# Adaptive max pool, 1-D: a fixed ring of 48 KB load slots and one extra load over 16 partitions, in place of slots that shrink from 64 KB to 48 KB

## The chip, the cores and the metric

One core of one Trainium2 chip. The metric is device microseconds of one execution. The kernel before was run three times: 335.7, 335.65 and 335.5 us, median 335.65 us. The profiled execution is one of its own kind: it took 335.7 us, of which 333.9 us are the span from its first instruction to its last.

## What is computed

`x` is 32 x 256 x 4096 float32 (134.2 MB), the output 32 x 256 x 256 float32 (8.4 MB). Each output is the maximum of 16 neighbouring inputs, since 4096 / 256 = 16:

```python
batch, channels, length = x.shape            # 32, 256, 4096
for i in range(output_size):                 # 256
    start = int(i * length / output_size)
    end = int((i + 1) * length / output_size)
    result[:, :, i] = np.max(x[:, :, start:end], axis=-1)
```

So `x` can be read as one long row of 2,097,152 windows of 16 floats (64 bytes), each of which gives one float (4 bytes).

## The kernel before

The long row of windows is cut into two groups, and each group into 128 equal pieces, one for each partition. A partition then owns 16,384 windows: 8,784 of the first group and 7,600 of the second. In what follows a "column" is one window on each of the 128 partitions: 64 bytes of each partition to load, 4 bytes to store.

A load (L74) brings some columns to one of three slots of the tile `area`; VectorE (DVE) reduces that slot with one `reduce_max` (L75) into the output part at the end of the same tile; the slot is then free for the third load after it. Memory of a partition is one area of 53,200 floats which slots and outputs share. The outputs grow downward from its end, and the slots get what is left, so they shrink: three loads each of 1,024, 980, 924, 868, 816 and 768 columns, and a last one of 244 (the loop at L43 to L50 works these sizes out). That is 19 loads. A load of 1,024 columns is 65,536 bytes to each partition, one of 768 columns is 49,152.

All DMAs are issued by SyncE (SP) in program order: 19 loads, then three stores (L91). The first store takes the whole first group (8,784 columns); the second takes the first six loads of the second group (5,052 columns), the third its last four loads (2,548 columns, L86 to L88). A load waits at SP until the reduce of the load three before it is done; the last store waits for the last reduce. VectorE does nothing but the 19 reduces, and the other engines compute nothing.

Of the kernel before, what the change touches and what calls it, by code (L numbers as in the profile page):

```python
# [1 line left out]

# [4 lines left out]


@with_exitstack
def kernel(  # L10
    ctx: ExitStack,
    tc: tile.TileContext,
    x: bass.AP,
    output_size: bass.AP,
    out: bass.AP,
):

    nc = tc.nc
    P = nc.NUM_PARTITIONS
    fp32 = mybir.dt.float32

    B, C, L = x.shape
    O = int(output_size)
    assert L % O == 0, (L, O)
    W = L // O
    total = B * C * O // P  # L30
    assert B * C * O % P == 0

    AREA = 53200
    SLOTS = 3
    MOST = 65536 // (4 * W)
    ALIGN = 4
    ROUNDS_A = 3
    LAST = 4


    sizes = []
    left = total
    while left:  # L43
        room = AREA - (total - left)
        n = min(room // (SLOTS * W + SLOTS) // ALIGN * ALIGN, MOST)
        for _ in range(SLOTS):
            n = min(n, left)
            if n:
                sizes.append(n)
                left -= n  # L50
    groups = [sizes[: ROUNDS_A * SLOTS], sizes[ROUNDS_A * SLOTS :]]

    pool = ctx.enter_context(tc.tile_pool(name="pool", bufs=1))
    area = pool.tile([P, AREA], fp32, tag="area", name="area")

    xw = x.flatten_outer_dims().rearrange("r (o w) -> (r o) w", w=W)
    ow = out.flatten_outer_dims().rearrange("r o -> (r o)")

    stores = []
    n_loads = 0  # L60
    first = 0
    low = AREA
    for g, loads in enumerate(groups):
        n = sum(loads)
        xg = xw[first : first + P * n].rearrange("(p n) w -> p (n w)", p=P)
        og = ow[first : first + P * n].rearrange("(p n) -> p n", p=P)
        first += P * n
        base = low - n
        b = n
        for i, size in enumerate(loads):  # L70
            a = b - size
            at = n_loads % SLOTS * sizes[n_loads // SLOTS * SLOTS] * W
            slot = area[:, at : at + size * W]
            nc.sync.dma_start(out=slot, in_=xg[:, a * W : b * W])  # L74
            nc.vector.reduce_max(  # L75
                out=area[:, base + a : base + b],
                in_=slot.rearrange("p (n w) -> p n w", w=W),
                axis=mybir.AxisListType.X,
            )
            n_loads += 1  # L80
            b = a
        low = base
        if g == 0:
            stores.append((og, area[:, base : base + n]))
        else:
            end = sum(loads[len(loads) - LAST :])  # L86
            for a, b in ((end, n), (0, end)):
                stores.append((og[:, a:b], area[:, base + a : base + b]))  # L88

    for dst, src in stores:  # L90
        nc.sync.dma_start(out=dst, in_=src)  # L91


# [1 line left out]
_INS = ['x', 'output_size']  # L95
_OUTS = [((32, 256, 256), 'float32')]

_NUMBERS = {'output_size': 256}


# [26 lines left out]
```

## Time and profile before

| what | value |
|---|---|
| median of three runs | 335.65 us |
| profiled execution, whole | 335.7 us |
| profiled execution, span of its instructions | 333.9 us |
| VectorE busy | 276.0 us (83% of the span), 19 reduces |
| VectorE idle before its reduces | 50.0 us, all of it waiting for a load |
| read from and written to device memory | 134.22 MB and 8.39 MB |
| mean rate over the span | 427 GB/s |

The DMA work of the core is done by 16 DMA engines. A DMA is cut into packets, which are spread over them; the profile counts packets, bytes and the share of the 16 engines' time that packets took. Each DMA tells its end with increments of a semaphore, one from each of the 16 engines, and the trace keeps the time of every one of them. A view by windows gives, for any stretch of time, what VectorE did and what the DMA engines moved; a packet is counted there whole in the window in which it starts.

### The profile page before, as it was taken

What the parts mean: (1) busy time and instruction counts of PE and PEld (TensorE: products, weight loads), DVE (VectorE), ACT (ScalarE), POOL (GpSimd) and SP (SyncE); (2) the same over time, 40 slices, a digit from 0 to 9 for tenths busy, and PEclk for the clock granted to TensorE, in tenths of its full rate; (3) what the DMA queues carried; (4) which work ended last, traced back from release to release, by engine and by line L of the source; (5) the groups of instructions that cost most, each with busy time, mean ns of one, the idle gap of its engine ahead of it and who ended that gap; (6) DMA issues with size and microseconds to landing.
All of it is one profiled execution on the core that took longest, in us unless ns stands there. A gap on an engine that the chain in (4) does not pass through costs nothing.

```text
span 333.9 us, 109 instructions
## 1 busy us (share of the span) xinstructions
DVE 276.0 (83%) x19; POOL 0.2 (0%) x4
## 2 busy tenths in 40 slices
DVE  0029899798979899897979897979989798988990
POOL 0000000000000000000000000000000000000000
DMA  9898989998999998999999999999999998998997
GB/s 377 377 502 377 495 385 471 392 473 376 473 443 398 474 439 383 425 453 453 446 426 433 426 426 426 426 425 469 407 419 475 395 465 389 465 436 383 448 420 311
DMA packets 3168, 142.61 MB, mean 427 GB/s; under 512 B 352, under 2 KB 352, under 8 KB 352
## 3 DMA queue, kind: packets, MB, share of 16 engines
q1 hardware_dynamic: 3168, 142.61, 99.1%
HBM read 134.22 MB, written 8.39 MB: 427 GB/s over the span
## 4 chain that ended last, share of the span: by engine, by line
DMA 63%; DVE 34%; another core or an unknown queue 1%; issue 0%; SPq 0%
DMA area<-in_x_dram 63%; DVE area L75 34%; SPq L74 0%
## 5 line engine op out<-in xcount | busy, mean ns | idle before, releaser
L75 DVE TENSOR_REDUCE area<-area 128x1024 f32<-128x16384 f32 (+6 forms) x19 | 276.0, 14525 | 50.0 <-DMA area<-in_x_dram 50.0
L108 POOL MEMSET const-bfloat16-1.0<- 128x1 bf16 x1 | 0.1, 102 | 0.0
L108 POOL MEMSET const-uint8-127<- 128x1 uint8 x1 | 0.1, 101 | 0.0
L108 POOL MEMSET const-float32-0.0<- 128x1 f32 x1 | 0.1, 100 | 0.2 <-issue 0.2
L108 POOL MEMSET const-float32-1.0<- 128x1 f32 x1 | 0.1, 99 | 0.0
## 6 DMA issues: line engine op xcount, KB each, us to landing
area<-in_x_dram SPq DMA_DIRECT2D x3, 7840.0 KB, 39.1
area<-in_x_dram SPq DMA_DIRECT2D x3, 7392.0 KB, 36.9
area<-in_x_dram SPq DMA_DIRECT2D x3, 6944.0 KB, 34.7
area<-in_x_dram SPq DMA_DIRECT2D x3, 6528.0 KB, 32.6
area<-in_x_dram SPq DMA_DIRECT2D x3, 6144.0 KB, 30.7
out_dram<-area SPq DMA_DIRECT2D x1, 4392.0 KB, 30.7
out_dram<-area SPq DMA_DIRECT2D x1, 2526.0 KB, 36.3
area<-in_x_dram SPq DMA_DIRECT2D x1, 1952.0 KB, 20.7
```

The lines of the kernel that those rows point to most:

```text
L75: nc.vector.reduce_max(out=area[:, base + a : base + b], in_=slot.rearrange("p (n w) -> p n w", w=W), axis=mybir.AxisListType.X,)
L108: nc = _bacc.Bacc("TRN2", target_bir_lowering=False, num_devices=1)
```

## The change

The shrinking slots are replaced by a ring of three slots of fixed size, 760 columns (48,640 bytes to each partition). Ahead of the two groups, 6,144 windows are taken off as a side piece: 16 partitions of 384 windows (24,576 bytes) each. The rest is 16,336 columns of 128 partitions, in groups of 7,600 and 8,736 columns: 10 loads of 760, then 11 of 760 and a last one of 376. The side load stands in the middle, as the twelfth of 23 (`SIDE_AT = 11` loads go before it). It is issued as two DMAs, one over 15 partitions and one over the sixteenth, and reduced by one instruction over 16 partitions. The columns are now walked from low to high. The stores are four: 7,600 columns, the side piece, 7,600 columns and 1,136 columns; the last one holds the last two loads. As built, SP has 24 load DMAs and 4 store DMAs where it had 19 and 3, and VectorE 23 reduces where it had 19. In the built program both sides of the sixteenth partition's DMA are one contiguous run of 6,144 floats: the `(k n)` view with `k=16` in the source does not survive the building.

```diff
-    AREA = 53200
     SLOTS = 3
-    MOST = 65536 // (4 * W)
-    ALIGN = 4
-    ROUNDS_A = 3
-    LAST = 4
...
-    while left:
-        room = AREA - (total - left)
-        n = min(room // (SLOTS * W + SLOTS) // ALIGN * ALIGN, MOST)
-        for _ in range(SLOTS):
-            n = min(n, left)
-            if n:
-                sizes.append(n)
-                left -= n
-    groups = [sizes[: ROUNDS_A * SLOTS], sizes[ROUNDS_A * SLOTS :]]
+    CHUNK = 760
+
+    SIDE_P, SIDE, SIDE_AT = 16, 384, 11
+    rest = (total - SIDE_P * SIDE) // P
+    GROUPS = [10 * CHUNK, rest - 10 * CHUNK]
+    CUT = 10 * CHUNK
...
-    area = pool.tile([P, AREA], fp32, tag="area", name="area")
+    ring = pool.tile([P, SLOTS, CHUNK * W], fp32, tag="ring", name="ring")
...
+    def next_slot(parts, n):
+        nonlocal n_loads
+        slot = ring[0:parts, n_loads % SLOTS, 0 : n * W]
+        n_loads += 1
+        return slot
+
+    def pooled(dst, src):
+        nc.vector.reduce_max(
+            out=dst,
+            in_=src.rearrange("p (n w) -> p n w", w=W),
+            axis=mybir.AxisListType.X,
+        )
+
+    def load(dst, src, a, b):
+        slot = next_slot(P, b - a)
+        nc.sync.dma_start(out=slot, in_=src[:, a * W : b * W])
+        pooled(dst[:, a:b], slot)
+
+    xs, os_ = group(SIDE_P, SIDE)
+    side_out = pool.tile([SIDE_P, SIDE], fp32, tag="side", name="side")
+
+    def load_side():
+        slot = next_slot(SIDE_P, SIDE)
+        last = SIDE_P - 1
+        nc.sync.dma_start(out=slot[0:last], in_=xs[0:last])
+        nc.sync.dma_start(
+            out=slot[last:SIDE_P].rearrange("p (k n) -> p k n", k=16),
+            in_=xs[last:SIDE_P].rearrange("p (k n) -> p k n", k=16),
+        )
+        pooled(side_out, slot)
...
+    for g, n in enumerate(GROUPS):
+        xg, og = group(P, n)
+        o = pool.tile([P, n], fp32, tag=f"out{g}", name=f"out{g}")
+        for a in range(0, n, CHUNK):
+            if n_loads == SIDE_AT:
+                load_side()
+            load(o, xg, a, min(a + CHUNK, n))
+        for a, b in ((0, CUT), (CUT, n)):
+            if a < b:
+                stores.append((og[:, a:b], o[:, a:b]))
+    assert taken == total
 
+    stores.insert(1, (os_, side_out))
     for dst, src in stores:
         nc.sync.dma_start(out=dst, in_=src)
```

More of the change, by code (lines that the diff above doesn't have):

```diff
@@ L29 @@
     W = L // O
-    total = B * C * O // P
-    assert B * C * O % P == 0
-    AREA = 53200
+    total = B * C * O
     SLOTS = 3
-    MOST = 65536 // (4 * W)
-    ALIGN = 4
-    ROUNDS_A = 3
-    LAST = 4
-    sizes = []
-    left = total
-    while left:
-        room = AREA - (total - left)
-        n = min(room // (SLOTS * W + SLOTS) // ALIGN * ALIGN, MOST)
-        for _ in range(SLOTS):
-            n = min(n, left)
-            if n:
-                sizes.append(n)
-                left -= n
@@ L57 @@
     ow = out.flatten_outer_dims().rearrange("r o -> (r o)")
-    stores = []
[L60 to L88, printed above, removed]
+    taken = 0
@@ new lines, in group @@
+    def group(parts, n):
+        nonlocal taken
+        span = slice(taken, taken + parts * n)
+        taken += parts * n
+        return (
+            xw[span].rearrange("(p n) w -> p (n w)", p=parts),
+            ow[span].rearrange("(p n) -> p n", p=parts),
+        )
+    n_loads = 0
+    def next_slot(parts, n):
[9 more added lines that the diff above has]
+        )
@@ new lines, in load @@
+    def load(dst, src, a, b):
[11 more added lines that the diff above has]
+            in_=xs[last:SIDE_P].rearrange("p (k n) -> p k n", k=16),
+        )
+        pooled(side_out, slot)
```

## The prediction

> **What bounds the kernel now.** I read the page's DMA queue first, because VectorE is 83% busy and some other thing must fill the rest.
>
> ```profile
> DMA packets 3168, 142.61 MB, mean 427 GB/s; under 512 B 352, under 2 KB 352, under 8 KB 352
> q1 hardware_dynamic: 3168, 142.61, 99.1%
> ```
>
> Packets fill 99.1% of the 16 engines' span, so the DMA engines bound the kernel. The count says how a DMA is cut: 22 DMAs x 128 partitions = 2,816 packets, and 22 x 16 = 352 tiny ones (the semaphore increments) make 3,168. So each partition's contiguous row was one packet, whether of 10 KB or 64 KB. The packet records add that a 65,536-byte packet takes 2.418 to 2.420 us in the steady state; 8 of them (128 rows / 16 engines) are 19.35 us.
>
> Next the timeline of VectorE, where each reduce starts 0.02 us after its load has landed.
>
> ```profile
> 42.33 17.22 DVE L75 TENSOR_REDUCE area<-area 128x1024 f32<-128x16384 f32 x1 [2.13 <-DMA area<-in_x_dram]
> 61.68 17.22 DVE L75 TENSOR_REDUCE area<-area 128x1024 f32<-128x16384 f32 x1 [2.13 <-DMA area<-in_x_dram]
> ...
> 279.80 12.95 DVE L75 TENSOR_REDUCE area<-area 128x768 f32<-128x12288 f32 x1 [0.85 <-DMA area<-in_x_dram]
> 293.16 33.20 SPq L91 DMA_DIRECT2D out_dram<-area  x3
> 294.26 12.95 DVE L75 TENSOR_REDUCE area<-area 128x768 f32<-128x12288 f32 x1 [1.51 <-DMA area<-in_x_dram]
> 308.79 17.21 DVE L75 TENSOR_REDUCE area<-area 128x768 f32<-128x12288 f32 x2 [1.57 <-DMA area<-in_x_dram]
> ```
>
> Landings are 61.68 - 42.33 = 19.35 us apart for 1,024 columns and 308.79 - 294.26 = 14.53 for 768. That is the packets' own time with nothing between, and VectorE idles before each reduce. The last reduce ends at 326.0 us (308.79 + 17.21); by the semaphore times the last three landings, all stores, are 10.46, 6.03 and 3.06 us apart (8,784, 5,052 and 2,548 columns), again the packets' own time. So the end is set by the slowest of 16 DMA engines, which after their first packet never idle: its first packet's end plus all its packets.
>
> Last, how far the engines lie apart, from windows around the second packets (one 65,536-byte packet starting in a 0.2 us window counts as 328 GB/s) and around the last ones (10,192 bytes in 0.1 us: 102 GB/s).
>
> ```profile
> 1.70:2.10 0.40, 0.00 (x0) 0.00 (x0) 1.00 8.29 2621
> 2.10:4.60 2.50, 0.00 (x0) 0.00 (x0) 1.00 0.00 0
> 4.60:4.80 0.20, 0.00 (x0) 0.00 (x0) 1.00 0.76 328
> 4.80:5.00 0.20, 0.00 (x0) 0.00 (x0) 1.00 2.27 983
> 5.00:5.20 0.20, 0.00 (x0) 0.00 (x0) 1.00 4.54 1966
> 5.20:5.40 0.20, 0.00 (x0) 0.00 (x0) 1.00 2.30 983
> 5.40:5.60 0.20, 0.00 (x0) 0.00 (x0) 1.00 1.51 655
> 5.60:5.80 0.20, 0.00 (x0) 0.00 (x0) 1.00 0.76 328
> ```
>
> ```profile
> 331.80:331.90 0.10, 0.00 (x0) 0.00 (x0) 1.00 0.49 204
> 331.90:332.00 0.10, 0.00 (x0) 0.00 (x0) 1.00 0.03 0
> 332.00:332.10 0.10, 0.00 (x0) 0.00 (x0) 1.00 0.26 102
> ```
>
> All 16 first packets start within 0.4 us, but the second ones start over 1 us: 1, 3, 6, 3, 2 and 1 of them. At the end two engines start their last packets at 331.8 to 331.9 and one alone 0.2 us later. The 16 increments of the last store come 0, 0.18, 0.19, 0.21, 0.39, 0.41, 0.42, 0.46, 0.47, 0.48, 0.50, 0.52, 0.59, 0.72, 0.75 and 0.97 us after the first. I call this an engine's lateness. Every landing of the run has the same pattern to 0.05 us: it arises in the first packet (2.84 to 3.80 us long) and is carried to the end. The trace doesn't number the engines.
>
> **The change, part by part.** All terms are time of one DMA engine.
>
> Columns. Landings fit 18.82 ns a column and 0.073 us a load: (19.35 - 14.53) / 256 columns, and 14.53 - 768 x 18.82 ns. They give 4.67 for the load of 244, whose landing is 4.67 after the one before. Stores: (10.46 - 3.06) / (8,784 - 2,548) = 1.19 ns a column, 0.035 a store. 48 columns leave the full-width stream: 48 x (18.82 + 1.19) ns = -0.96. Three loads more of full width (22 for 19): +0.22. Three big stores stay three. Sum -0.74.
>
> Side pieces. 24,576 bytes at 18.82 ns / 512 bytes (8 rows of 64) are 0.90, with some 0.01 for a descriptor 0.92 us: an estimate from those rows. The side store, 16 rows of 1,536 bytes, one an engine: 0.07. How pieces are dealt decides. Fifteen rows over 15 engines, one each, follows the way 128 rows became 8 each; the far bound is all 15 on one engine, 13.8 us. I take one each. The sixteenth row is one contiguous run in the built program, and every contiguous run of the trace was one packet; I take one packet of 0.92 on one engine. Bounds: a sixteenth of it (0.06 with its overhead 0.08) on each if it is split after all; or 0.92 on the one engine left free, which makes all even. Since 15 of 16 engines have a piece already, I take it as a second piece on one of them. Then, against before:
> - 14 engines: -0.74 + 0.92 + 0.07 = +0.25
> - one engine: -0.74 + 1.84 + 0.07 = +1.17
> - one engine: -0.74 + 0.07 = -0.67.
>
> The end moves by the largest of (lateness + term) less 0.97. The one with two pieces is late by anything of the list: its end moves by +0.20 (lateness 0) to +1.17 (lateness 0.97). The 14: at most +0.25, or 0.75 + 0.25 - 0.97 = +0.03 if the latest engine is the one relieved. I choose a lateness of 0.37, the mean of the five engines whose first packets started earliest (0.39, 0.23, 0.52, 0.47, 0.21 at the end of their first packets), supposing that the engine served first also gets a lone piece: 0.37 + 1.17 - 0.97 = +0.57.
>
> [...]
>
> VectorE. A reduce costs (12.95 - 4.22) / (768 - 244) = 16.66 ns a column whatever the partitions, so 12.82 for 760, 6.42 for 376 and 6.55 for the side piece. Total 21 x 12.82 + 6.42 + 6.55 = 282.2, that is 6.2 more, at no cost as long as slots come free in time: 50.0 us of idle hide it. A slot's load (load n+3) is issued 12.87 us after load n landed, with n+1 and n+2, 28.8 us of packets, ahead of it. That cover is gone at one place. The two loads ahead of load 13 (counted from 0; it waits for reduce 10) are the side load and load 12, so its descriptors, at 12.87 plus 1.02 to 1.30 (issue at 0.73 of the span to the first packets at 1.7 to 2.1), come 13.9 to 14.2 us after load 10. An engine has 0.92 + 14.38 = 15.3 us of work then, less its lead of up to 0.97. It just fits for the 14 and for the one with two pieces; the relieved one waits. If a restart costs the extra of a first packet again (0.43 to 1.38 us) the 14 go from +0.25 to some +0.4, below the doubled engine's +0.57. Taken as 0. The side reduce then delays reduce 12 by 5 us and the loads behind find 10 us of cover.
>
> Tail. After the last load lands, stores of 9.05 + 0.07 + 9.05 = 18.2 us are queued; the last two reduces end 12.82 + 6.42 - 7.15 = 12.1 us after it. The last store still finds the DMA engines busy: nothing gained or lost.
>
> Sum: 335.7 (profiled, span 333.9 and 1.8 around it) + 0.57 = 336.27; against the median of the runs, 335.65, it is 336.2.
>
> **The rivals.** A change of 0.2%, 0.67 us, is about what a measurement of this kernel can tell from none.
>
> *The doubled engine is a late one (slower).* With lateness over 0.47 its end moves by 0.67 to 1.17: 336.3 to 336.8. For it: 7 of 16 engines are that late. Against: it needs the lone piece to fall on one of them. It decides from lateness 0.47.
>
> *The sixteenth is spread, or falls on the free engine (no change).* Split, the 15 engines move by +0.33 and the sixteenth by -0.59: end +0.11 if the relieved engine is the latest, +0.33 if not; on the free engine all move by +0.25. 335.75 to 336.0. Against: the contiguous run in the built program, and one engine in sixteen.
>
> *Dealing or restart is worse than taken (slower).* Fewer engines for 15 rows (three pieces on each of five: 1.84 us more than +0.25) or a dry queue at load 13: 337 and up to 349 by the 13.8. Against: the even dealing of 128 rows.
>
> *Faster.* Would need 0.67 off all late engines. First packets of 48,640 bytes in place of 65,536 could shrink the largest extra of 1.38 in proportion, by 0.35; with +0.03 for a relieved latest engine and an even side the end comes 0.3 earlier: 335.35, still within 0.2%.
>
> **How the numbers follow.** Forecast (double piece, moderate lateness, +0.2 to +0.67) 0.46; late doubled engine 0.28; spread or even 0.13; worse dealing or restart 0.08; faster than thought 0.05, which I give to faster by over 0.2%, for a reason I don't see. Slower: 0.28 + 0.08 = 0.36, rounded up to 0.37 for cases at the edge; within 0.2%: 0.58. The range goes from the spread case, 335.7, to the late doubled engine and a little restart, 336.9; it leaves out the two tails.
>
> **What would show it.** 3,232 packets of data (25 DMAs of 128 rows = 3,200, and 15 + 1 + 16 rows) beside the increments; a single 24,576-byte packet for the sixteenth; landings 14.38 us apart; after the side load the gap between the latest and the next engine wider, the last store's spread over 1.2 us; no idle DMA time around load 13. Wrong it would be if the 15 rows take more than one packet on an engine, if the side load's landing comes much over 2 us after load 10's, or if the first packets' lateness is another.

## The result and the profile after

The changed kernel takes 340.04 us (median of six runs, 339.33 to 340.85), the kernel before on the same chip 335.67 (335.42 to 335.87): ratio 1.0131, 95% interval 1.0116 to 1.0146. It is 4.4 us slower. The profiled execution took 340.25 us with a span of 338.5.

From the page of the changed kernel, its head, the DMA counts and the reduces:

```profile
span 338.5 us, 117 instructions
...
DMA packets 3664, 142.61 MB, mean 421 GB/s; under 512 B 432, under 2 KB 448, under 8 KB 576
...
q1 hardware_dynamic: 3664, 142.61, 98.7%
...
L67 DVE TENSOR_REDUCE out<-ring 128x760 f32<-128x12160 f32 (+1 forms) x22 | 275.5, 12528 | 48.1 <-DMA ring<-in_x_dram 48.1
L67 DVE TENSOR_REDUCE side<-ring 16x384 f32<-16x6144 f32 x1 | 6.5, 6529 | 0.0
```

The reader sees the same bytes, and DMA engines still booked for 98.7% of the span, but at 421 GB/s in place of 427. Packets that are in flight count as busy whether they move fast or slowly, so a busy share near 100% hides a slow stretch: of the page's 40 slices the one that moved 288 GB/s counts as busy for 90% or more, like its neighbours at 397 and 448. The timeline of VectorE shows where that stretch lies:

```profile
132.91 12.82 DVE L67 TENSOR_REDUCE out<-ring 128x760 f32<-128x12160 f32 x1 [1.57 <-DMA ring<-in_x_dram]
...
147.28 12.82 DVE L67 TENSOR_REDUCE out<-ring 128x760 f32<-128x12160 f32 x1 [1.56 <-DMA ring<-in_x_dram]
...
163.29 12.82 DVE L67 TENSOR_REDUCE out<-ring 128x760 f32<-128x12160 f32 x1 [3.19 <-DMA ring<-in_x_dram]
176.03 6.53 DVE L67 TENSOR_REDUCE side<-ring 16x384 f32<-16x6144 f32 x1
182.49 12.80 DVE L67 TENSOR_REDUCE out<-ring 128x760 f32<-128x12160 f32 x1
195.73 12.82 DVE L67 TENSOR_REDUCE out<-ring 128x760 f32<-128x12160 f32 x1 [0.45 <-DMA ring<-in_x_dram]
```

Loads land 14.37 us apart (147.28 - 132.91), as predicted for 760 columns. Load 10, the one ahead of the side load, lands 16.01 us after load 9 (163.29 - 147.28): already the load in front of it is 1.6 us late. By the packet records its last data packet ended on time, at 161.68; what came late are its increments, the last of them at 163.27. Two loads of 760 and one side piece should bring load 13 to 163.29 + 0.92 + 28.76 = 193.0; it lands at 195.7. All is lost around the side load; behind it the distance is 14.38 again to the end. The view by windows (length, VectorE's busy time, GpSimd's, clock, DMA share, and GB/s last; the side load's first packet starts at 160.48) gives the depth of it:

```profile
146.20:160.40 14.20, 12.82 (x1) 0.00 (x0) 1.00 0.98 421
160.40:163.40 3.00, 0.11 (x1) 0.00 (x0) 1.00 1.43 253
163.40:166.20 2.80, 2.80 (x1) 0.00 (x0) 1.00 0.61 183
166.20:180.40 14.20, 14.20 (x2) 0.00 (x0) 1.00 1.00 428
```

In 5.8 us the engines move 253 x 3.0 + 183 x 2.8 = 1,271 KB, for which 428 GB/s needs 3.0 us: 2.8 us are gone there. The other 1.6 us are that the engines no longer lie together: the sixteen increments of a DMA were spread over 0.70 us before the side load and over 2.33 us from then to the end. The packet records say which packets: the sixteen of 24,576 bytes took 1.95 to 3.24 us, where 0.92 was predicted, and the first packet of the load behind them 2.3 to 4.6 us (one 2.1) where 1.80 is usual.

### The profile page after: what moved, and what is told of

The parts are those of the page before. It is cut to its first block, busy times and chain, and to the rows that moved or that the text cites. A ratio compares the mean times of both kernels' runs of the same rounds, so it can differ in the third digit from the quotient of the medians.

```text
span 338.5 us, 117 instructions
## 1 busy us (share of the span) xinstructions
DVE 281.9 (83%) x23; POOL 0.2 (0%) x4
## 3 DMA queue, kind: packets, MB, share of 16 engines
q1 hardware_dynamic: 3664, 142.61, 98.7%
## 4 chain that ended last, share of the span: by engine, by line
DMA 63%; DVE 30%; issue 3%; DVEq 2%; SPq 0%
DMA ring<-in_x_dram 63%; DVE out L67 28%; DVE side L67 2%; DVEq L137 2%; SPq L75 0%
## 5 line engine op out<-in xcount | busy, mean ns | idle before, releaser
L67 DVE TENSOR_REDUCE out<-ring 128x760 f32<-128x12160 f32 (+1 forms) x22 | 275.5, 12528 | 48.1 <-DMA ring<-in_x_dram 48.1
L67 DVE TENSOR_REDUCE side<-ring 16x384 f32<-16x6144 f32 x1 | 6.5, 6529 | 0.0
```

The costliest lines, as they stand in the source:

```text
L67: nc.vector.reduce_max(out=dst, in_=src.rearrange("p (n w) -> p n w", w=W), axis=mybir.AxisListType.X,)
```

## The experiments

All times are medians. "Before" is the kernel before on the same chip as the runs of that group: 335.58 for the first group, 335.53 for the second, 335.59 for the third, 335.60 for the last. "Place of its own" means the part of the second group's output tile that is written much later; "ring" is a ring slot as in the change.

| run | side load | where | us | ratio to before, 95% interval |
|---|---|---|---|---|
| change | 15 + 1 rows, partitions 0 to 15 | ring | 340.04 | 1.0131 (1.0116 to 1.0146) |
| e1 | none | | 335.78 | 1.0007 (0.9998 to 1.0017) |
| e2 | 16 rows, 0 to 15 | ring | 338.81 | 1.0095 (1.0078 to 1.0112) |
| e3 | 16 rows, every 7th | ring | 339.22 | 1.0109 (1.0094 to 1.0124) |
| e4 | 15 + 1 rows, 0 to 15 | own | 339.91 | 1.0127 (1.0112 to 1.0142) |
| e5 | 32 partitions | ring | 339.20 | 1.0099 (1.0081 to 1.0116) |
| e6 | 64 partitions | ring | 338.45 | 1.0088 (1.0073 to 1.0103) |
| e7 | 128 partitions | ring | 337.97 | 1.0071 (1.0056 to 1.0086) |
| e8 | 120 partitions | ring | 338.87 | 1.0102 (1.0084 to 1.0119) |
| e9 | 128 partitions | own | 335.85 | 1.0008 (0.9999 to 1.0018) |
| e10 | 16 rows, 0 to 15 | own | 338.96 | 1.0109 (1.0092 to 1.0126) |
| e11 | 16 rows, every 7th | own | 336.69 | 1.0035 (1.0022 to 1.0048) |
| e12 | 120 partitions | own | 337.49 | 1.0055 (1.0040 to 1.0070) |
| e13 | 16 rows, every 2nd | own | 337.09 | 1.0047 (1.0032 to 1.0062) |
| e14 | 32 partitions | own | 336.97 | 1.0041 (1.0026 to 1.0055) |
| e15 | 64 partitions | own | 336.81 | 1.0039 (1.0025 to 1.0054) |

**First group: four suspects.** A: sixteen engines that write sixteen neighbouring partitions crowd each other. B: the load behind the side load is issued with too little work ahead of it (too little cover). Then the source of the side load, and the second piece on one engine.

e1, the ring without the side load:

```diff
-    SIDE_P, SIDE, SIDE_AT = 16, 384, 11
-    rest = (total - SIDE_P * SIDE) // P
+    rest = total // P
...
-            if n_loads == SIDE_AT:
-                load_side()
...
-    stores.insert(1, (os_, side_out))
```

> The ring of three slots of 760 columns alone: no side load, all 16,384 columns over 128 partitions (21 loads of 760, one of 424; stores of 7,600, 7,600 and 1,184). If the 4.4 us come from the side load and its neighbourhood (both theories below), this takes about the time before: +0.22 us for three more loads, and about -0.28 because the engines' spread after the first packet was 0.71 us in the changed kernel and 0.99 before: 335.6 us. If the ring of smaller packets itself costs, it stays at 338 us or more.

Measured 335.78, 0.20 us over the kernel before, with an interval of the ratio that takes in no change at all (0.9998 to 1.0017). That is what its three loads more should cost; the 0.28 us that the expectation took off for a smaller spread of the engines didn't come (its own profile spreads by 0.95 us, not by 0.71). The whole rest, 340.04 - 335.78 = 4.3 us, belongs to the side load.

e2, one DMA over 16 partitions:

```diff
-        nc.sync.dma_start(out=slot[0:last], in_=xs[0:last])
-        nc.sync.dma_start(
-            out=slot[last:SIDE_P].rearrange("p (k n) -> p k n", k=16),
-            in_=xs[last:SIDE_P].rearrange("p (k n) -> p k n", k=16),
-        )
+        nc.sync.dma_start(out=slot, in_=xs)
```

> The side load as one DMA over its 16 partitions, in place of 15 and 1. Theory A (crowding: sixteen engines writing into sixteen neighbouring partitions get in each other's way, and what follows queues behind): 16 packets still take 2 to 3.2 us in place of 0.92, the next load's first packets still 2.3 us and more; only the second piece of one engine goes, which kept it some 0.9 us behind the next at the end: 338.8 to 339.3 us. Theory B (cover: the load behind the side load is issued so late that the queue runs dry): same 338.8 to 339.3, the cover is the same. If the second piece on one engine were most of it, 336.5 us or less.

Measured 338.81: 1.2 us less than the change. The second piece on one engine is real, and it is the smaller part; 3.0 us over e1 remain.

e3, the same rows at every seventh partition (`STEP = 7`, `HIGH = 16 * STEP`):

```diff
-        slot = next_slot(SIDE_P, SIDE)
-        nc.sync.dma_start(out=slot, in_=xs)
+        slot = next_slot(HIGH, SIDE)
+        nc.sync.dma_start(out=slot[0:HIGH:STEP], in_=xs)
```

> The same one DMA of 16 rows, but its rows go to partitions 0, 7, 14 to 105 in place of 0 to 15 (the reduce then runs over 112 partitions, of which those 16 are stored; it takes the same time). Theory A: the packets take 0.92 to 1.9 us, and the next load's first packets near 1.80 us: 335.9 to 336.8 us. Theory B: the side packets get shorter too or not, but the load behind is issued as late as before and its first packets still take 2.3 us and more: 337.5 to 339 us. A third theory, that reading sixteen neighbouring rows of 24,576 bytes from memory is the slow part: no change against the 16-partition DMA, 338.8 to 339.3 us.

Measured 339.22, which by the expectations speaks for the third theory, and wrongly. Its timeline shows a new wait:

```profile
159.97 0.33 SPq L75 DMA_DIRECT2D ring<-in_x_dram  x1
161.50 12.82 DVE L67 TENSOR_REDUCE out<-ring 128x760 f32<-128x12160 f32 x1 [1.56 <-DMA ring<-in_x_dram]
174.35 0.59 SPq L85 DMA_DIRECT2D ring<-in_x_dram  x1
174.99 24.13 SPq L75 DMA_DIRECT2D ring<-in_x_dram  x3
179.49 6.55 DVE L67 TENSOR_REDUCE side<-ring 112x384 f32<-112x6144 f32 x1 [5.17 <-DMA ring<-in_x_dram]
```

The side load (L85) is issued only at 174.35, when the reduce that began at 161.50 has ended: it waited for the reduce of load 10, which is in another slot, as if its rows with gaps between them overlapped the whole ring. So the queue ran dry, and VectorE stood 5.17 us. The run says nothing on the source. Its side packets took 0.99 to 1.68 us, though, which points at A, but weakly, since no other load was under way when they started.

e4, the change with the side load in a place of its own:

```diff
-        slot = next_slot(SIDE_P, SIDE)
+        slot = o[0:SIDE_P, o.shape[1] - SIDE * W : o.shape[1]]
```

> The changed kernel, with the side load in a place of its own (the part of the second group's output tile that is written much later) in place of a ring slot. It waits for no reduce and takes no slot, so that the load behind it is issued with two full loads ahead, as everywhere else. Theory A: the side packets still take 2 to 3.2 us and the next packets are slow too: 339 to 340 us. Theory B: the next load's first packets take 1.80 us; what is left is the side packets' own 1 to 2.3 us extra and the second piece: 337.5 to 338.3 us; if the side packets were slow for want of work behind them too, 336.2 us.

Measured 339.91, as the change within the runs' spread. With the rows at partitions 0 to 15, giving back the cover buys nothing.

**Second group: the same bytes over more partitions, in the ring.** Only `SIDE_P, SIDE` differ from e2: 32 x 192, 64 x 96, 128 x 48, and 120 x 48 (5,760 windows; the main stream has 16,339 columns then).

> The same 393,216 bytes of the side load, read from the same place, as one DMA over 32 partitions of 192 windows (12,288 bytes a row, two rows an engine). [...] Source theory (neighbouring rows in device memory are slow to read): 338.8 us, the bytes are the same.

> The same bytes over 64 partitions of 96 windows (6,144 bytes a row). [...] Source theory: 338.8 us. [...]

> The same bytes over all 128 partitions, 48 windows each (3,072 bytes a row, eight rows an engine). Theory A: no crowding, packets of 3,072 bytes take some 0.12 us each and the next load's first packets 1.80 us: 335.8 to 336.1 us, the time without a side load and 0.1 to 0.2 for one load and one store more. Theory B (the load behind a short load is issued too late): the loads around it are issued as in the 16-partition form, so 1 to 2 us stay: 337 us or more. Source theory: 338.8 us.

> A side load over 120 partitions of 48 windows, as one DMA (the main stream keeps 16,339 columns). [...]

Measured 339.20, 338.45, 337.97 and 338.87. Over 128 partitions, where A alone would give 335.8 to 336.1, the side load still costs 2.2 us over e1. The timeline of e7:

```profile
160.09 32.25 SPq L75 DMA_DIRECT2D ring<-in_x_dram  x4
161.67 12.82 DVE L67 TENSOR_REDUCE out<-ring 128x760 f32<-128x12160 f32 x1 [1.61 <-DMA ring<-in_x_dram]
174.40 0.94 DVE L67 TENSOR_REDUCE side<-ring 128x48 f32<-128x768 f32 x1
179.16 12.82 DVE L67 TENSOR_REDUCE out<-ring 128x760 f32<-128x12160 f32 x1 [3.82 <-DMA ring<-in_x_dram]
```

Load 10 lands on time (161.67) and the side load too, but load 12 lands 17.5 us after load 10 (179.16 - 161.67) in place of 0.9 + 14.4 = 15.3. It was issued at 160.09. By the packet records three engines, done with the side load by 162.2, stood idle until load 12's first packet at 162.91, 162.95 and 163.67, and those took 2.5 to 2.7 us in place of 1.80. That is B, at full price. In e5 and e6 it is not load 12 but load 13, which also has only the side load and one full load ahead of it, that comes late. In e5:

```profile
178.22 12.82 DVE L67 TENSOR_REDUCE out<-ring 128x760 f32<-128x12160 f32 x1
194.46 12.82 DVE L67 TENSOR_REDUCE out<-ring 128x760 f32<-128x12160 f32 x1 [3.41 <-DMA ring<-in_x_dram]
```

These are the reduces of loads 12 and 13, 16.24 us apart in place of 14.38. By the packet records one engine was done with load 12 at 177.39 and got its first packet of load 13 at 178.66; that packet took 2.86 us. Since lost cover is in every run of this group, at one load or the other, its steps from 16 to 128 partitions don't price the crowding.

**Third group: the two causes apart.** The first line is that of e9; e10 and e11 have 16 and 384 there, e12 has 120 and 48. A place of its own, one load earlier, so that the side load is issued without any wait and the load behind has two full loads ahead; e11 also fills the place with zeros beforehand, since its reduce reads all 112 partitions. All four load the side piece with one DMA, as e2 does.

```diff
-    SIDE_P, SIDE, SIDE_AT = 16, 384, 11
+    SIDE_P, SIDE, SIDE_AT = 128, 48, 10
...
-        slot = next_slot(SIDE_P, SIDE)
+        slot = o[0:SIDE_P, o.shape[1] - SIDE * W : o.shape[1]]
```

> The side load over all 128 partitions again, but in a place of its own (in the second group's output tile, as one load earlier than before so that it waits for nothing), so that the load behind it has two full loads and the side load ahead of it when it is issued. Theory B (cover) says that the 2.2 us of the 128-partition side load in a ring slot (337.97 against 335.78 without) came from the load behind it, which was issued with only 1.3 us more work ahead than its first packets needed: 335.8 to 336.0 us here, no engine idle around the side load. If a short load costs this by itself, wherever it is put, 337.5 to 338.0 us.

> The 16-partition side load (one DMA, partitions 0 to 15) in a place of its own. The cover is whole, so what is left over the run with 128 partitions in the same place is the crowding alone. Theory A: side packets of 2 to 3.2 us, the next packets slow as well, 338.0 to 338.9 us. Theory B alone: 335.9 to 336.2 us.

> The same 16 rows, read from the same place, put into the same place of partitions 0, 7, 14 to 105 (the place is filled with zeros by GpSimd long before, so that the reduce over 112 partitions reads nothing unset). [...] Source theory, or sixteen single rows being slow wherever they go: as with partitions 0 to 15, 338.0 to 338.9 us. [...]

> The 120-partition side load in a place of its own: relief of one engine by 24,576 bytes with neither crowding nor lost cover. If the relieved engine is the run's latest, its gain shows against the 128-partition load in the same place: 0.2 to 0.4 us less. If lateness falls on another engine, the same time or 0.05 us more.

e9 takes 335.85: with all partitions and whole cover a short load in the middle is free (0.07 us over none). So B is worth 337.97 - 335.85 = 2.1 us by itself. e10 takes 338.96: with whole cover, partitions 0 to 15 cost 3.1 us. e11, the same rows from the same source at every seventh partition, takes 336.69: that is 2.3 us off, and it clears the source. The windows of e10, from the side load's first packet on:

```profile
146.10:148.90 2.80, 0.63 (x1) 0.00 (x0) 1.00 1.39 245
148.90:151.60 2.70, 2.70 (x1) 0.00 (x0) 1.00 0.60 180
```

The same of e11:

```profile
146.10:148.90 2.80, 1.42 (x1) 0.00 (x0) 1.00 1.30 418
148.90:151.60 2.70, 2.70 (x1) 0.00 (x0) 1.00 0.79 342
```

And of e9:

```profile
146.00:148.90 2.90, 1.69 (x1) 0.00 (x0) 1.00 1.05 438
148.90:151.60 2.70, 2.70 (x1) 0.00 (x0) 1.00 1.25 540
```

e10 repeats the change's dip (245 and 180 GB/s against 253 and 183) though nothing was issued late; e11 has a shallower one, e9 none. (Packets count whole at their start, so a window can show more than the engines' rate.)

e12 takes 337.49, 1.6 us more than e9: the relief of one engine, which its expectation takes as given, shows no gain. Its side packets took up to 0.39 us where those of e9 took 0.12 to 0.13.

**Last group: how many partitions, or which ones.** e13 is e11 with `STEP = 2`; e14 and e15 are e9 with 32 x 192 and 64 x 96.

> The 16 rows to partitions 0, 2, 4 to 30, in a place of their own. [...] If any 16 rows within one part of the memory crowd alike, 338.5 to 339 us.

> The same bytes over partitions 0 to 31 (two rows of 12,288 bytes an engine), in a place of their own. [...] By the number of partitions: a third to a half of the cost of 16 (3.1 us over 128 partitions): 337.0 to 337.4 us. [...]

> The same bytes over partitions 0 to 63 (four rows of 6,144 bytes an engine), in a place of their own. [...] By the number of partitions: 336.2 to 336.4 us, a clear step below 32. [...]

Measured 337.09, 336.97 and 336.81. If any 16 rows within one part of the memory crowded alike, e13 would take 338.5 to 339 us; by the number of partitions alone e15 would take 336.2 to 336.4, a clear step below e14. Neither came. Sixteen rows spread over partitions 0 to 30 cost what 32 partitions cost, and 64 are within the runs' spread of 32, while 128 give back a whole microsecond (335.85). The packet records show it more sharply: from the first to the last moment of the side packets 3.9 us pass at partitions 0 to 15, 2.8 at every second one, 2.8 with 32, 2.6 with 64, 2.1 at every seventh, 1.6 with 128 (0.6 of it the engines' own spread). So the time follows which partitions are written, and not their number alone: sixteen rows took 338.96 us at partitions 0 to 15, 337.09 at every second one and 336.69 at every seventh. Why these differ, no run shows.

## Why the prediction was wrong

It forecast 336.2 us, no change that can be told, with a range of 335.7 to 336.9; measured are 340.04, 3.1 us above the range's upper end.

*The step that failed* is the price of a side piece: "24,576 bytes at 18.82 ns / 512 bytes (8 rows of 64) are 0.90, with some 0.01 for a descriptor 0.92 us: an estimate from those rows". Those rows are loads over 128 partitions; none of them has sixteen engines writing a few neighbouring partitions at once. The size of a packet was scaled and its destination forgotten. Sixteen such packets into partitions 0 to 15 took 1.95 to 3.24 us, and the packets behind them were slow too. e2 over e1 prices that: 3.0 us in the ring; e10 over e9: 3.1 us with cover. I gave both bounds for how the pieces are dealt to engines, and none for where they are written. Its own sign of being wrong came: the side load landed 4.0 us after load 10 (163.27 to 167.27), where "much over 2 us" was to say so.

*The second weak step* was the cover: a restart was "Taken as 0" because the work ahead "just fits". It says that cover is gone "at one place", load 13; there are two. Load 12, the first behind the side load, has by the same arithmetic the same 15.3 us ahead of it. Load 12 came late in e7, load 13 in e5. The first packets' delay after an issue, 1.02 to 1.30 us in the profile before, was taken as the delay in the middle of a stream; e7 shows 2.8 to 3.6 us on the late engines. The price is 2.1 us (e7 against e9). In the time of the changed kernel it doesn't show: e10 and e2 differ by less than their spread, as do e4 and the change. Its load 12 is issued as late (160.13), but only one engine waits for it, 0.42 us, until 162.10: the slow side packets keep the others occupied, and that seems to hide the late issue. Taking away either cause alone leaves 2 to 3 us; taking away both leaves 335.85.

*What was right.* The ring: sum of +0.22 us for three loads, 0.20 measured in e1. Landings 14.38 us apart. The sixteenth row as one packet on an engine that had one already: sixteen packets of 24,576 bytes, of which fifteen start between 160.48 and 161.47 us and one at 163.63; and 432 increments, 26 DMAs x 16 and 15 + 1, so that the two side DMAs ran on 15 engines and on one. Its term of 0.92 us measures 1.2 (change against e2) and 0.95 (e4 against e10). VectorE's longer work stayed hidden (281.9 us busy against 276.0, 5.9 more where 6.2 were predicted), and so did the tail. The last store's increments spread over 2.31 us, "over 1.2" as foretold, and by its cause: in e2, without the second piece, they spread over 1.00. The mean of the five latenesses is 0.36, not 0.37, which is nothing in the sum.

*The sum, as measured*: ring 0.20 + side load over partitions 0 to 15 3.03 (e2 less e1) + second piece 1.23 (change less e2) = 4.46. As a chain of differences it closes on 340.04 - 335.58 by design, which checks nothing; beside its own runs of the kernel before (335.67) the change costs 4.37. Each term has its own run.

*The latest engine.* The lateness list of the profile before was used as if it belonged to the kernel. The change and the experiments all begin with the same packets of 48,640 bytes, and at the first load's landing their profiles spread by 0.44 us (e11) to 0.96 (e2): it is no property of the kernel. The four runs on one chip (e1 to e4) go from 0.55 to 0.96, so it isn't the chip's either. So relief of one fixed engine has nothing steady to win, as far as one profile of each can say; e12, which was meant to give that relief with the cover whole, is slower than e9 (337.49 against 335.85).

None of the runs beats the kernel before. e1 and e9 come within 0.3 us of it, and the intervals of both take in no change.

## What to carry to other kernels

When DMA engines bound a kernel, a transfer's price is not bytes over rate alone: the same 393,216 bytes took the kernel to 338.96 us at partitions 0 to 15 and to 335.85 over all 128 (e10, e9). Ask which partitions it writes, and whether several engines now write the same few at once. A narrow load can stall the wide ones behind it, so its cost can be larger than its own length: 3.1 us here for a piece of 0.92. And count how much work is queued ahead of each load when it is issued: a short load takes the place of a long one there (2.1 us here, e7 against e9), and two causes that overlap have to be removed together before the time comes back.

## What the runs showed that was not expected

The stall is not limited to the partitions of the side load. The next load writes all 128, and yet in e10 all sixteen of its first packets end between 5.46 and 6.02 us after the first side packet started, whenever they began (2.06 to 3.92 us after it): they seem to move only as the last side packets drain (3.9 us). That one slow write holds up what is behind it on other engines is a reading of these times; no run here looks inside it.

A DMA doesn't have to be narrow for it. In e12, with a DMA over 120 partitions, packets took up to 0.39 us where those over 128 partitions took 0.13 at most, and it cost 1.6 us (337.49 against 335.85). The loss is at the side load: from the landing of load 8 to that of the load behind the side load 31.2 us pass (133.12 to 164.28), where e9 takes 29.7 (132.80 to 162.54). Why 120 partitions cost more than 128 wasn't tried apart.
